# A decoder block on one Trainium2 core: one more column turned by DMA instead of TensorE, and the first turned tile of the mixer's norm joined one weight unit later

## The chip, the cores and the metric

The kernel runs on one core of one Trainium2 chip, and nothing else of the chip is used. The metric is the device time of one execution in microseconds (us); a comparison uses the median of several runs. The core has a matrix engine (TensorE, PE in the profile; PEld is its weight load), a vector engine (VectorE, DVE), an activation engine (ScalarE, ACT), GpSimd (POOL) and SyncE (SP). SP's queue issues all the large transfers. Each engine works through its own instructions in order and waits on semaphores that the others raise.

## The reference, cut to what matters

One layer, batch 1, 256 tokens, model width 2048, feed-forward width 5632, all in float32. `x` is the residual.

```python
def swiglu_ffn(x, w_gate, w_up, w_down):
    return (jax.nn.silu(x @ w_gate) * (x @ w_up)) @ w_down

x = x + 0.5 * swiglu_ffn(rms_norm(x, ffn1_norm), ffn1_w_gate, ffn1_w_up, ffn1_w_down)
z = rms_norm(x, mix_norm) @ w_in                 # 2048 -> 5120 columns
...                                              # RG-LRU branch and short convolution on z
y = concatenate([rms_norm(y_lru, lru_out_norm), rms_norm(y_sc, sc_out_norm)])
x = x + y @ w_out                                # 2048 -> 2048
x = x + 0.5 * swiglu_ffn(rms_norm(x, ffn2_norm), ffn2_w_gate, ffn2_w_up, ffn2_w_down)
return rms_norm(x, final_norm)
```

The change concerns two of these norms: `mix_norm` (called `nm` in the kernel) and `ffn2_norm` (`n2`). Each takes the finished residual, which lies with tokens on the partitions, and needs it turned, with the model dimension on the partitions, because the matrix engine contracts over partitions.

## The kernel before, in words

**Tiling.** The residual `xres` is held on chip as two tiles of 128 tokens (`t` = 0, 1) by 2048 columns, thought of as four columns of 512 (`c` = 0 to 3). A weight unit is a 512 x 512 block of a weight matrix, loaded by one 1 MB transfer from SP's queue (`load`) and cut into a high part (a cast on ACT, `hi_...`, in two halves of 128 x 1024) and a low part (a subtraction on DVE, `lo_...`); three high/low pairs are in use in turn. For two token tiles a unit takes 24 matmuls of 512 columns on PE: 16 with the high part, 8 with the low part. That is done in `multiply`, which ends with a call of `onward()` whenever it works on two targets. The two feed-forward layers use a seven-product scheme (`seven`), and their down projections end with `add_units(3, ...)`.

**Turning a column of the residual.** It is done in one of two ways. `Norm.turn` uses PE: for each of the four blocks of 128 columns two transposes into PSUM (`pt_...`), then one scaling on ACT and one fused multiply-subtract on DVE, which write the high and low part of the turned column `xT_...`. `Norm.cross` uses DMA and is done for each token tile in two steps: `begin` has ACT copy the tile into one side of `pair` as 16-bit halves, and SP issue a transposing DMA from there into a free tile (`cross_...`); `store` has ACT copy the result back (`join`, "COPY pair<-cross" in the trace), and then four scalings on ACT and four multiply-subtracts on DVE write `xT_...`. `pair` has two sides, so two tiles are under way at most.

**What sets the order.** The `cross` tasks lie in the queue `tasks`. Each `onward()`, so each weight unit with two targets, finishes the tile that is under way (`store`) and begins the next one. `Norm.later` puts columns 0 to 2 into that queue and column 3 into `pending` as a `turn` by PE. `pump` and `flush` work `pending` off. Outside a pinned opening, a scheduler reorders the instructions of each engine as it expects them to be ready, so the order on the engines differs from the written one; `join` alone is kept in program order.

**The two places.** The first is the end of the first feed-forward layer, in its last `down`: while the last units of `w_down` (tiles `raw_d1_9_...`) are multiplied, the finished columns of the residual go through `cross_nm_c_t`; `u3` and `s5` there are copies of PSUM sums that ACT takes (`snap`), and PE may reuse a PSUM bank only after such a copy. The mixer's input projection `columns` (sums `ps_in`) follows, and its first unit is followed by the transposes `pt_nm` of column 3. The second place is the start of the second feed-forward layer (`begin_after`): it multiplies four units of `w_gate` and four of `w_up` in turn (`ps_g`, `ps_u`), the first two with `xT` of column 0, the last two with column 3. Column 3 of the residual is complete only after the last unit of `w_out`, right before that loop, and its transposes `pt_n2_12` to `pt_n2_15` stand between the first `ps_g` and the first `ps_u` unit.

Of the kernel before, what the change touches and what calls it, by code (L numbers as in the profile page):

```python
# [12 lines left out]
U16 = mybir.dt.uint16  # L13
# [6 lines left out]
S = 256  # L20
FF = 5632
NT = S // P
KD = D // P
KF = FF // P
CW = 512
NC_D = D // CW
# [23 lines left out]
def hybrid_block(ctx: ExitStack, tc: tile.TileContext, a: dict, out: bass.AP):  # L50
# [3 lines left out]
    x = a["x"][0]  # L54
# [5 lines left out]
    def defer(cost, fn):  # L60
        pending.append((cost, fn))
# [24 lines left out]
    def f32(ap):  # L86
        return ap.bitcast(F32)
# [62 lines left out]
    def big(name):  # L150

        return bigs.tile([P, UK, 2 * S], F32R, tag="big", name=name)
# [42 lines left out]
    def stationary(tile, t):  # L195

        return [(tile[:, j, t * P : (t + 1) * P], tile[:, j, S + t * P : S + (t + 1) * P]) for j in range(UK)]

    mixed, flat = "p (f b) -> p b f", "p (b f) -> p b f"
    pair = const.tile([P, NT, CW], F32, name="pair")  # L200
    tasks, moving, sides = deque(), deque(), [0]

    def part(src, turned):

        sides[0] = 1 - sides[0]
        two = pair[:, sides[0]].bitcast(U16)
        act.copy(two.rearrange(flat, b=2), src.bitcast(U16).rearrange(mixed, b=2))
        nc.sync.dma_start(turned.rearrange("p (r c) -> p r c", c=P), two, transpose=True)
        return pair[:, sides[0]]

    def join(two, turned):
        tc.keep_in_program_order(act.copy(two.bitcast(U16).rearrange(mixed, b=2), turned.rearrange(flat, b=2)))
        return quad(two)

    def onward():

        if moving:
            two, _, fn = moving.popleft()
            fn(two)
        if tasks:  # L220
            key, begin, fn = tasks.popleft()
            moving.append((begin(), key, fn))

    def on_the_way():
        return {task[0] for task in tasks} | {entry[1] for entry in moving}
# [18 lines left out]
    class Norm:  # L244
# [27 lines left out]

        def cross(self, c, t, room):
            x = xres[:, t, c * CW : (c + 1) * CW]
            place = []

            def begin():
                place.append(room(f"cross_{self.name}_{c}_{t}").bitcast(U16))
                return part(x, place[0])

            def store(two):
                v = join(two, place[0])
                if t == 0:
                    self.xT[c] = big(f"xT_{self.name}_{c}")
                for j in range(UK):
                    g = self.gain[:, UK * c + j : UK * c + j + 1]
                    hi, lo = (self.xT[c][:, j, o + t * P : o + (t + 1) * P] for o in (0, S))
                    act.activation(hi, v[:, j], AF.Copy, scale=g)
                    dve.scalar_tensor_tensor(lo, v[:, j], g, f32(hi), op0=ALU.mult, op1=ALU.subtract)

            tasks.append(((self.name, c), begin, store))

        def later(self, c, room):
            if c < NC_D - 1:
                for t in range(NT):
                    self.cross(c, t, room)
            else:
                defer(1.6, lambda: self.turn(range(4 * c, 4 * c + 4)))
            defer(0.1, lambda: self.squares(c))

# [98 lines left out]
    def quad(tile):  # L399
        return tile.rearrange("p (j c) -> p j c", j=UK)  # L400
# [76 lines left out]
    def ffn(tag, norm, after, opening=False):  # L477
        with (
# [37 lines left out]
            def plain(u, x=None):  # L516

                x = f32(norm.xT[u] if x is None else x)
                for t, v in room(u).items():
                    dve.tensor_tensor(  # L520
                        v, x[:, :, t * P : (t + 1) * P], x[:, :, S + t * P : S + (t + 1) * P], op=ALU.add
                    )
# [26 lines left out]
            def first_columns(m, u, **how):  # L549
                return load(ws[m][u * UK * P : (u + 1) * UK * P, :CW], f"{m}{tag}_0_{u}", **how)  # L550
# [136 lines left out]
            def begin_after():  # L687
                follow = {
                    (0, "g"): [flush],
                    (0, "u"): [norm.factor, lambda: plain(0)],  # L690
                    (1, "g"): [lambda: norm.rows(keep), lambda: plain(1), lambda: normalise(0)],
                    (1, "u"): [lambda: normalise(1), sums, lambda: plain(2)],
                    (2, "g"): [lambda: normalise(2), lambda: plain(3)],
                }
                for u in range(KD // UK):
                    for m in "gu":
                        assert (norm.name, u) not in on_the_way()
                        blk = parts_of(first_columns(m, u), f"{m}{tag}_0_{u}")
                        multiply([(ps[m, t], stationary(norm.xT[u], t), u == 0, u == 3) for t in range(NT)], blk)
                        pump(1.5)  # L700
                        for fn in follow.get((u, m), ()):
                            fn()
                units.append(big(f"x{tag}_3"))
                for t in range(NT):
                    sg = keep(f"sg{tag}_0_{t}")
                    act.activation(sg, ps["g", t], AF.Silu, scale=norm.r[:, t : t + 1])
                    dve.scalar_tensor_tensor(
                        sg, ps["u", t], norm.r[:, t : t + 1], sg, op0=ALU.mult, op1=ALU.mult
                    )
                    turn_hidden(0, t, sg, False)  # L710
# [152 lines left out]
    nm = held["nm"]  # L863


    with tc.tile_pool(name="mixer", bufs=1) as mp, tc.tile_pool(name="mixw", bufs=2) as mw:
# [18 lines left out]
        def tmp(tag, name, w=S, dt=F32, bufs=2):  # L885
            return mw.tile([P, w], dt, tag=tag, name=f"{tag}_{name}", bufs=bufs)
# [179 lines left out]
        n2 = Norm("n2", vec["ffn2_norm"])  # L1066
        w_out = a["w_out"][0]
        rs = []
        for c in range(NC_D):
            cs = slice(c * CW, (c + 1) * CW)  # L1070
            for g in range(2):
                if c == 0 and g == 1:
                    flush()
                ps = product(w_out, c, (2 * g, 2 * g + 1), yT.__getitem__, f"o{c}_{g}")
                if c == 0:
                    pst = bank(f"pst_{g}")
                    for t in range(NT):
                        pe.matmul(
                            pst[:, t : t + 1], acc[:, g, t * P : (t + 1) * P], ones[:, :1], start=True, stop=True
                        )  # L1080
                    tot = work.tile([P, NT], F32, tag="tot", name=f"tot_y{g}")
                    dve.tensor_copy(tot, pst[:, :NT])
                    rs.append(inv_sqrt(tot, D // 2, f"y{g}"))
                for t in range(NT):
                    xr = xres[:, t, cs]
                    dve.scalar_tensor_tensor(xr, ps[t], rs[g][:, t : t + 1], xr, op0=ALU.mult, op1=ALU.add)
            n2.later(c, lambda name: tmp("T", name, 4 * S)[:, :CW])


    fss = const.tile([P, NT, NC_D + 1], F32, name="fss")  # L1090
# [87 lines left out]
```

## Time and profile before

| | before |
|---|---|
| median of 3 runs | 1715.81 us (1714.99 to 1716.85) |
| the profiled execution's own time | 1715.85 us |
| its span, first to last instruction | 1713.7 us |
| granted TensorE clock | 0.999 |
| busy, share of the span: PE, PEld | 99%, 82% |
| busy, share of the span: DVE, ACT | 86%, 68% |
| weight transfers, bytes in all, mean rate | 357.91 MB, 209 GB/s |

The profiled execution took 2.15 us more than its span, and 0.04 us more than the median. Busy shares are means over stages. A row of the timeline reads: start in us, time in us, engine, line, operation, output<-inputs, form, count, and in brackets the idle time before it with what ended it. A merged row of several matmuls ends later than the next row starts, because matmuls overlap in the pipeline; the pace of PE is therefore read from one row's start to the next row's start. The profile leaves numbers out of names: `xT_n` of the second layer is `xT_n2`, and `u_d` is one of `u2`, `u3`.

### The profile page before, as it was taken

The page shows a single profiled execution, that of the slowest core. Times are in us where ns is not written, and L with a number is a line of the kernel's source. Part 1 is how long each engine was busy: PE and PEld are TensorE (multiplying, and loading weights), DVE is VectorE, ACT ScalarE, POOL GpSimd, SP SyncE. Part 2 cuts the span into 40 slices and gives each one's busy share as a digit, 9 for nine tenths or more (in the row PEclk, how much of TensorE's full clock was granted, in tenths as well). Part 3 has the DMA queues.
Part 4 walks back from the last instruction along what each step waited for, and adds up shares of the span by engine and source line. Part 5 has one row for each costly group of instructions (what it writes and reads, how often), then busy time and mean ns, then how long its engine had stood idle before and what let it go on. Part 6 is the DMA issues. An engine that isn't in the chain of part 4 may idle for free.

```text
span 1713.7 us, 20224 instructions
## 1 busy us (share of the span) xinstructions
PE 1695.6 (99%) x7811; PEld 1412.7 (82%) x7811; DVE 1479.7 (86%) x1293; ACT 1164.8 (68%) x1481; POOL 6.9 (0%) x32
## 2 busy tenths in 40 slices
PE   8999999999999999999999999999999999999997
PEld 6888888888888887888888888888888888888886
DVE  7998988879889878787987679979989888889796
ACT  6767667776567678875665766686667765677764
POOL 1000000000000000000000000000000000000000
PEclk9999999999999999999999999999999999999999
DMA  8666567585567685755555784695666656576753
GB/s 299 206 220 198 196 221 221 184 268 200 183 209 208 227 264 135 248 172 195 175 195 173 221 278 142 205 269 187 225 202 218 225 186 221 196 215 202 251 192 123
DMA packets 233056, 357.91 MB, mean 209 GB/s; under 512 B 64772, under 2 KB 67200, under 8 KB 232832
## 3 DMA queue, kind: packets, MB, share of 16 engines
q1 hardware_dynamic: 232496, 355.50, 63.8%
q8 instruction: 61, 1.00, 0.2%
q10 hardware_dynamic: 144, 1.05, 0.1%
q14 instruction: 35, 0.29, 0.1%
q0 software_dynamic: 320, 0.07, 0.0%
HBM read 339.82 MB, written 2.10 MB: 200 GB/s over the span
## 4 chain that ended last, share of the span: by engine, by line
PE 75%; ACT 3%; DVE 2%; DMA 0%; issue 0%; DVEq 0%; SPq 0%; ACTq 0%
PE ps_in L43 13%; PE ps_d L43 12%; PE ps_u_a L43 7%; PE ps_g_a L43 6%; PE ps_o L43 5%; PE ps_u_c L43 5%; PE ps_d_a L43 4%; PE ps_g_c L43 3%; PE ps_g_d L43 3%; PE ps_u_d L43 3%; PE ps_d_c L43 2%; PE ps_u_e L43 2%; PE ps_d_d L43 2%; PE ps_g_e L43 2%; PE ps_u L43 1%; PE ps_g L43 1%
## 5 line engine op out<-in xcount | busy, mean ns | idle before, releaser
L43 ACT CAST hi_u_p<-raw_u 128x1024 fp32r<-128x1024 f32 x140 | 141.5, 1047 | 55.7 <-DVE raw_u L43 25.4
L43 ACT CAST hi_g_p<-raw_g 128x1024 fp32r<-128x1024 f32 x132 | 133.9, 1047 | 57.5 <-DVE raw_g L43 30.0
L43 DVE TENSOR_TENSOR lo_u_p<-raw_u,hi_u_p 128x2048 fp32r<-128x2048 f32 (+1 forms) x80 | 159.9, 2018 | 14.4 <-ACT hi_u_p L43 13.8
L43 DVE TENSOR_TENSOR lo_g_p<-raw_g,hi_g_p 128x2048 fp32r<-128x2048 f32 (+1 forms) x75 | 151.6, 2031 | 19.1 <-ACT hi_g_p L43 18.5
L43 PE MATMUL ps_d<-hi_d,h 128*128 128x512 f32 x704 | 167.0, 389 | 0.0
L43 PEld LDWEIGHTS ps_d<-hi_d,h 128*128 128x128 f32 x704 | 132.1, 188 | 27.4
L43 PE MATMUL ps_in<-xT_nm,hi_in 128*128 128x512 f32 x640 | 153.2, 391 | 0.0
L43 PEld LDWEIGHTS ps_in<-xT_nm,hi_in 128*128 128x128 f32 x640 | 117.4, 188 | 23.1 <-ACT tha L43 0.3
L43 ACT CAST hi_d_p<-raw_d 128x1024 fp32r<-128x1024 f32 x84 | 86.1, 1048 | 64.1 <-DVE raw_d L43 24.2
L43 DVE TENSOR_TENSOR lo_d<-raw_d,hi_d 128x2048 fp32r<-128x2048 f32 x44 | 100.2, 2288 | 29.9 <-ACT hi_d L43 29.7
L43 ACT CAST hi_in<-raw_in 128x1024 fp32r<-128x1024 f32 x80 | 80.0, 1045 | 57.5 <-PE ps_in L43 44.5
L43 DVE TENSOR_TENSOR lo_in<-raw_in,hi_in 128x2048 fp32r<-128x2048 f32 x40 | 91.2, 2285 | 31.0 <-ACT hi_in L43 30.6
L43 DVE TENSOR_TENSOR lo_d_p<-raw_d,hi_d_p 128x2048 fp32r<-128x2048 f32 (+1 forms) x48 | 96.5, 2020 | 10.8 <-ACT hi_d_p L43 10.3
L43 ACT CAST hi_u_x<-raw_u 128x1024 fp32r<-128x1024 f32 x80 | 81.3, 1046 | 35.2 <-PE ps_u_c L43 24.9
L43 ACT CAST hi_d<-raw_d 128x1024 fp32r<-128x1024 f32 x88 | 88.9, 1046 | 20.0 <-PE ps_d_d L43 7.6
L43 DVE TENSOR_TENSOR raw_u<-raw_u,raw_u 128x2048 f32<-128x2048 f32 (+1 forms) x50 | 92.3, 1862 | 10.8 <-DMA raw_u<-in_ffn_w_up_dram 10.3
L43 DVE TENSOR_TENSOR lo_g_x<-raw_g,hi_g_x 128x2048 fp32r<-128x2048 f32 x40 | 91.4, 2285 | 8.7 <-ACT hi_g_x L43 8.7
L43 ACT CAST hi_g_x<-raw_g 128x1024 fp32r<-128x1024 f32 x80 | 81.2, 1046 | 21.3 <-PE ps_g_c L43 8.6
L43 DVE TENSOR_TENSOR lo_u_x<-raw_u,hi_u_x 128x2048 fp32r<-128x2048 f32 x40 | 91.4, 2284 | 1.4 <-ACT hi_u_x L43 1.1
L43 DVE TENSOR_TENSOR raw_g<-raw_g,raw_g 128x2048 f32<-128x2048 f32 (+1 forms) x46 | 84.9, 1868 | 5.4 <-DMA raw_g<-in_ffn_w_gate_dram 4.9
L43 PE MATMUL ps_d<-lo_d,h 128*128 128x512 f32 x352 | 87.3, 389 | 0.0
L43 PEld LDWEIGHTS ps_in<-xT_nm,lo_in 128*128 128x128 f32 x640 | 82.1, 191 | 3.1
(406 smaller groups left out, 3669.2 us busy)
## 6 DMA issues: line engine op xcount, KB each, us to landing
raw_d<-in_ffn_w_down_dram SPq DMA_DIRECT2D x88, 1024.0 KB, 5.7
raw_u<-in_ffn_w_up_dram SPq DMA_DIRECT2D x87, 1024.0 KB, 5.3
raw_g<-in_ffn_w_gate_dram SPq DMA_DIRECT2D x86, 1024.0 KB, 5.4
raw_in<-in_w_in_dram SPq DMA_DIRECT2D x40, 1024.0 KB, 5.1
raw_o<-in_w_out_dram SPq DMA_DIRECT2D x16, 1024.0 KB, 5.1
xres<-in_x_dram SPq DMA_DIRECT2D x4, 512.0 KB, 7.7
raw_u<-in_ffn_w_up_dram SPq DMA_DIRECT2D x2, 512.0 KB, 9.5
raw_g_first<-in_ffn_w_gate_dram SPq DMA_DIRECT2D x1, 1024.0 KB, 12.2
```

The lines of the kernel that those rows point to most:

```text
L43: ins = getattr(self.engine, name)(*args, **kwargs)
```

## The change

Three edits. `onward()` skips one call for the very first tile of the mixer's norm (key `("nm", 0)`, seen once): at the unit where that tile would be joined nothing is done, and it and every later tile of the norm come one unit later. `Norm.cross` takes its free tile when the task is queued, no longer when it begins. For `n2`, column 3 is no longer turned on PE: `later` gets `last=False` and leaves out the deferred `turn`, and `begin_after` queues two `cross` tasks for it before its first unit.

```diff
-    tasks, moving, sides = deque(), deque(), [0]
+    tasks, moving, sides, seen = deque(), deque(), [0], set()
...
     def onward():
 
+        if moving and moving[0][3]:
+            moving[0][3] = False
+            return
         if moving:
-            two, _, fn = moving.popleft()
+            two, _, fn, _ = moving.popleft()
             fn(two)
         if tasks:
             key, begin, fn = tasks.popleft()
-            moving.append((begin(), key, fn))
+            moving.append([begin(), key, fn, key == ("nm", 0) and key not in seen])
+            seen.add(key)
...
         def cross(self, c, t, room):
             x = xres[:, t, c * CW : (c + 1) * CW]
-            place = []
+            place = room(f"cross_{self.name}_{c}_{t}").bitcast(U16)
 
             def begin():
-                place.append(room(f"cross_{self.name}_{c}_{t}").bitcast(U16))
-                return part(x, place[0])
+                return part(x, place)
...
-        def later(self, c, room):
+        def later(self, c, room, last=True):
             if c < NC_D - 1:
                 for t in range(NT):
                     self.cross(c, t, room)
-            else:
+            elif last:
                 defer(1.6, lambda: self.turn(range(4 * c, 4 * c + 4)))
             defer(0.1, lambda: self.squares(c))
...
+                for t in range(NT):
+                    norm.cross(NC_D - 1, t, keep)
                 for u in range(KD // UK):
                     for m in "gu":
...
-            n2.later(c, lambda name: tmp("T", name, 4 * S)[:, :CW])
+            n2.later(c, lambda name: tmp("T", name, 4 * S)[:, :CW], False)
```

At the first place, on ACT, before (`cross_nm_0_0` is column 0, token tile 0; `x00`, `p3`, `x10` are three successive weight units; `u3` is a copy of a PSUM sum):

```order
L43 CAST hi_d1_9_p2_4857<-raw_d1_9_101_4684 128x1024
L43 COPY pair_107<-cross_nm_0_0_4772 128x2x512
L43 ACTIVATE xT_nm_0_4825<-pair_107,cols_many_94 128x128 x4
L43 CAST hi_d1_9_x00_4879<-raw_d1_9_70_4688 128x1024 x2
L43 COPY pair_107<-cross_nm_0_1_4834 128x2x512
L43 CAST hi_d1_9_p3_4921<-raw_d1_9_90_4678 128x1024
L43 COPY u3_d1_9_4855<-ps_d1_9_a_4674 128x512
L43 ACTIVATE xT_nm_0_4825<-pair_107,cols_many_94 128x128 x4
```

and now, on ACT at the same place:

```order
L43 CAST hi_d1_9_p2_4845<-raw_d1_9_101_4686 128x1024
L43 CAST hi_d1_9_x00_4869<-raw_d1_9_70_4690 128x1024 x2
L43 COPY pair_107<-cross_nm_0_0_4674 128x2x512
L43 ACTIVATE xT_nm_0_4899<-pair_107,cols_many_94 128x128 x4
L43 CAST hi_d1_9_p3_4911<-raw_d1_9_90_4680 128x1024
L43 COPY u3_d1_9_4843<-ps_d1_9_a_4676 128x512
L43 CAST hi_d1_9_p3_4911<-raw_d1_9_90_4680 128x1024
L43 CAST hi_d1_9_x10_4928<-raw_d1_9_80_4694 128x1024 x2
L43 COPY pair_107<-cross_nm_0_1_4675 128x2x512
```

The two casts of unit `x00` now stand ahead of the first join, and the second join stands behind the copy `u3` and the casts of `x10`, no longer ahead of `u3`.

At the same place on SP's queue, now (before, `cross_nm_0_1` stood right behind `cross_nm_0_0`, and `cross_nm_1_1` right behind `cross_nm_1_0`, each ahead of the weight unit that precedes it now):

```order
L165 DMA raw_d1_9_100_4692<-in_ffn1_w_down_dram 128x4x512
L208 DMA_TRANSPOSE cross_nm_0_0_4674<-pair_107 128x8x128
L165 DMA raw_d1_9_80_4694<-in_ffn1_w_down_dram 128x4x512
L208 DMA_TRANSPOSE cross_nm_0_1_4675<-pair_107 128x8x128
L165 DMA raw_d1_9_3_10_4989<-in_ffn1_w_down_dram 128x4x512
L208 DMA_TRANSPOSE cross_nm_1_0_4867<-pair_107 128x8x128
L165 DMA raw_d1_9_3_9_5044<-in_ffn1_w_down_dram 128x4x512
L208 DMA_TRANSPOSE cross_nm_1_1_4868<-pair_107 128x8x128
```

Two transposing DMAs of this place have moved behind a weight transfer; none was added.

At the second place on PE, before (`ps_g2`, `ps_u2` are the sums of the second layer's first gate and up columns):

```order
L43 MATMUL ps_g2_0_1_8016<-lo_g2_0_0_8022,xT_n2_0_7595 128x512 x4
L43 MATMUL pt_n2_12_8050<-ident_77,xres_76 128x128 x2
L43 MATMUL pt_n2_13_8056<-ident_77,xres_76 128x128 x2
L43 MATMUL pt_n2_14_8061<-ident_77,xres_76 128x128 x2
L43 MATMUL pt_n2_15_8066<-ident_77,xres_76 128x128 x2
L43 MATMUL ps_u2_0_0_8017<-hi_u2_0_0_8077,xT_n2_0_7595 128x512 x8
```

The four rows `pt_n2` are gone from PE, and nothing takes their place there. On ACT, at the same place, now:

```order
L43 COPY pair_107<-xres_76 128x1024
L43 ACTIVATE junk_n2_3_0_8054,ss_n2_7338<-xres_76 128x512
L43 COPY pair_107<-xres_76 128x1024
L43 ACTIVATE junk_n2_3_1_8056,ss_n2_7338<-xres_76 128x512
L43 CAST hi_g2_0_1_8120<-raw_g2_0_1_8118 128x1024
L43 ACTIVATE s_n2_8104<-v_n2_8103 128x2
L43 CAST hi_g2_0_1_8120<-raw_g2_0_1_8118 128x1024
L43 CAST hi_u2_0_1_8179<-raw_u2_0_1_8177 128x1024
L43 COPY pair_107<-cross_n2_3_0_8019 128x2x512
L43 COPY pair_107<-cross_n2_3_1_8020 128x2x512
L43 ACTIVATE xT_n2_3_8090<-pair_107,cols_many_94 128x128 x8
L43 CAST hi_u2_0_1_8179<-raw_u2_0_1_8177 128x1024
```

ACT gained two copies into `pair`, two joins and eight scalings of 128 x 128, and lost four of 128 x 256; the second half of the cast of the second up unit (`hi_u2_0_1`) now stands behind the joins. SP's queue carries the two transposing DMAs between the transfers of `raw_u2_0_1` and `raw_g2_0_2`.

2 lines of the change are left out of this document (1 added, 1 removed).

## The prediction

> **What bounds the kernel now.** I read the page first: the span, the busy shares and the chain that ended last.
>
> ```profile
> span 1713.7 us, 20224 instructions
> PE 1695.6 (99%) x7811; PEld 1412.7 (82%) x7811; DVE 1479.7 (86%) x1293; ACT 1164.8 (68%) x1481; POOL 6.9 (0%) x32
> ```
>
> PE is busy 99%, but busy time alone doesn't say that it is the bound, so next I asked what PE waits for over the whole span (columns: waiter, releaser, us in total, times, longest):
>
> ```profile
> PE pt_n L43 <- DMA xres<-in_x_dram: 3.1, 1, 3.1
> ...
> PE ps_g_a L43 <- DVE lo_g_p L43: 1.4, 4, 0.4
> ...
> PE ps_d_a L43 <- ACT u_d L43: 0.4, 1, 0.4
> ```
>
> After the opening (its longest wait is the 3.1 us), PE waits for nobody longer than half a microsecond at a time. So time is saved only by taking instructions off PE or by removing one of these small waits, and lost only by a new wait of PE. Work added on ACT, DVE or DMA costs nothing until PE waits for it. The last row is at the first place of the change. The chain of waits there, in order of time:
>
> ```profile
> 658.77 8.30 DMA cross_nm<-pair
> ...
> 667.10 1.36 ACT pair L43
> ...
> 673.72 0.58 ACT u_d L43
> ...
> 674.35 2.11 PE ps_d_a L43 x8
> ```
>
> It leaves PE: a transposing DMA takes 8.30 us to land, ACT's join waits for it, everything behind the join on ACT is late, the copy `u_d` among it, and PE stands for that copy.
>
> **The first place: the join one unit later.** ACT's timeline there, then PE's:
>
> ```profile
> 661.79 1.05 ACT L43 CAST hi_d_p<-raw_d 128x1024 fp32r<-128x1024 f32 x1
> 667.10 1.35 ACT L43 COPY pair<-cross_nm 128x1024 uint16<-128x1024 uint16 x1 [4.25 <-DMA cross_nm<-pair]
> ...
> 669.67 1.98 ACT L43 CAST hi_d_x<-raw_d 128x1024 fp32r<-128x1024 f32 x2
> ```
>
> ```profile
> 664.69 1.07 PE L43 MATMUL ps_d_e<-lo_d_x,h 128*128 128x512 f32 x4
> ...
> 666.51 1.98 PE L43 MATMUL ps_d_a<-hi_d_p,hs 128*128 128x512 f32 x8
> ...
> 674.35 2.11 PE L43 MATMUL ps_d_a<-hi_d_x,h 128*128 128x512 f32 x8 [0.42 <-ACT u_d L43]
> ...
> 689.33 3.79 PE L43 MATMUL ps_d<-hi_d,h 128*128 128x512 f32 x16
> ...
> 694.77 3.79 PE L43 MATMUL ps_d<-hi_d,h 128*128 128x512 f32 x16
> ```
>
> The loss is larger than the 0.42 us in brackets, because an interruption also shows as longer steps. The pace is 0.2267 us a matmul: 689.33 to 694.77 is 5.44 us for 24. From 666.51 to 689.33 stand 96 matmuls of 512 columns, that is 21.77 us at this pace, and it took 22.82. So PE loses 1.05 us in this stretch, and that is the most the first edit can bring.
>
> Would it? Now ACT has the casts of unit `x00` between 661.79 and the join. They need the high part of three units earlier, which PE has read by 664.69, so they run from about 664.9 to 666.8, inside the hole of 4.25 us. The join then starts at 667.10 as before, the scalings end at 669.67, the first cast of `p3` at 670.6 and the copy `u3` (one of `u_d`) at 671.1 instead of 674.3. PE wants it at 673.8. What was late is early by more than 2 us, so I take the full 1.05 us. The bounds: 1.05 from above, and from below nothing, or a loss, if the delayed tasks are late at the mixer. The new late candidates come from two transposes now behind a weight transfer on SP's queue. SP's row there (two weight units from 665.19 on), and the landings of the six transposes of this norm:
>
> ```profile
> 665.19 9.17 SPq L165 DMA_DIRECT2D raw_d<-in_ffn_w_down_dram  x2
> ```
>
> ```profile
> DMA to landing us min/median/max: 2.8/4.1/8.3
> ```
>
> The second tile's transpose goes out about 665.6, right behind `raw_d1_9_80`. Even the 8.30 us just seen would land it at 673.9, and its join comes up on ACT at 673.9 by the same durations; behind it the casts of `p1` have until 685.5 on PE. The added wait is thus near nothing; behind it on ACT stand those casts and the two copies for column 1, and DVE's low parts wait for the casts.
>
> At the mixer's start the delayed tasks meet a tight place. SP's, ACT's, DVE's and PE's rows:
>
> ```profile
> 696.05 3.13 SPq L208 DMA_TRANSPOSE cross_nm<-pair  x2
> ```
>
> ```profile
> 700.38 2.57 ACT L43 COPY pair<-cross_nm 128x1024 uint16<-128x1024 uint16 x2 [1.23 <-DMA cross_nm<-pair]
> ```
>
> ```profile
> 704.93 0.69 DVE L43 SCALAR_TENSOR_TENSOR xres<-ps_d,xres 128x512 f32<-128x512 f32 x1
> ```
>
> ```profile
> 703.83 2.08 PE L43 MATMUL ps_in<-xT_nm,lo_in 128*128 128x256 f32 x16
> 705.75 1.03 PE L43 MATMUL pt_nm<-ident,xres 128*128 128x128 f32 x8
> ```
>
> The transposes `pt_nm` read a residual column that DVE finishes at 705.62, queued behind work that waits for ACT's joins of column 2: PE comes at 705.75, only 0.1 us behind. If PE arrives 1.05 us earlier, at 704.70, DVE must be earlier too. Walked through the new order with the same durations, ACT's two copies for column 2 end near 692.7 and 695.2 (the hole of 4.25 us is filled now); before, SP had its first issue only at 696.05. So the second transpose goes out near 695.4, and with the 4.3 us that 696.05 to 700.38 shows it lands near 699.7. One join, one scaling, two multiply-subtracts and the two residual updates are about 3.4 us more: ready at 703.1, with 1.6 us to spare. I keep the full 1.05 for the sum.
>
> **The second place: column 3 of `n2` by DMA.** PE's rows:
>
> ```profile
> 1023.57 1.03 PE L43 MATMUL pt_n<-ident,xres 128*128 128x128 f32 x8
> 1024.36 3.89 PE L43 MATMUL ps_u<-hi_u,xT_n 128*128 128x512 f32 x16
> 1028.08 1.98 PE L43 MATMUL ps_u<-lo_u,xT_n 128*128 128x512 f32 x8
> ...
> 1035.71 3.88 PE L43 MATMUL ps_u<-hi_u,xT_n 128*128 128x512 f32 x16
> ```
>
> The eight transposes hold PE from 1023.57 to 1024.36, 0.79 us, and the 16 matmuls after them take 3.72 instead of 16 x 0.2267 = 3.63, so 0.09 more. Both go: 0.88 us. The Trainium skill ("VectorE: DVE Perf Modes", The three transpose paths) gives 390 ns for a 128x128 transpose on TensorE against 1309 ns by DMA and advises TensorE if PSUM will do as the destination. That advice speaks against this change; by its figure the eight would be an estimated 3.1 us on PE, and the sum below 4.2 instead of 1.93. The rows have 0.79 us for eight, and they decide.
>
> What is added must hide beside PE. Rows for its prices (durations in ns, least/median/most), and ACT's timeline where it goes:
>
> ```profile
> L208 SPq DMA_TRANSPOSE T_cross_n<-pair x6: 1231/1238/1259, 958.7 to 999.3; - x6
> L43 ACT COPY pair<-T_cross_n x6: 1342/1348/1360, 961.7 to 1004.5; 128x1024 uint16<-128x1024 uint16 x6
> DMA to landing us min/median/max: 2.7/2.8/3.2
> L43 ACT ACTIVATE xT_nm<-pair,cols_many x24: 384/388/402, 668.5 to 704.9; 128x128 fp32r<-128x128 f32 x24
> L43 DVE SCALAR_TENSOR_TENSOR xT_nm<-pair,cols_many,xT_nm x24: 341/347/354, 668.9 to 706.3; 128x128 fp32r<-128x128 f32 x24
> L43 DVE SCALAR_TENSOR_TENSOR xT_n<-pt_n,cols_many,xT_n x4: 473/474/477, 1025.6 to 1026.8; 128x256 fp32r<-128x256 f32 x4
> ```
>
> ```profile
> 996.65 1.04 ACT L43 COPY pair<-xres 128x1024 uint16<-128x1024 uint16 x1
> ...
> 1018.41 0.63 ACT L43 ACTIVATE junk_n<-xres 128x512 f32<-128x512 f32 x1
> ...
> 1024.48 1.56 ACT L43 ACTIVATE xT_n<-pt_n,cols_many 128x256 fp32r<-128x256 f32 x4
> 1028.28 2.00 ACT L43 CAST hi_g<-raw_g 128x1024 fp32r<-128x1024 f32 x2 [2.24 <-PE ps_u L43]
> 1033.72 1.99 ACT L43 CAST hi_u<-raw_u 128x1024 fp32r<-128x1024 f32 x2 [3.44 <-PE ps_g L43]
> 1039.13 0.62 ACT L43 CAST x<-v 128x512 fp32r<-128x512 f32 x1 [3.42 <-DVE v L43]
> ```
>
> ACT: 2 x 1.04 + 2 x 1.35 + 8 x 0.39 - 1.56 = +6.3 us. It fits into the 2.24 + 3.44 + 3.42 = 9.1 us in which ACT waits here. DVE: 8 x 0.347 - 4 x 0.474 = +0.9 us, beside a PE that waits for none of it. SP: two issues of 1.24 us; `raw_g2_0_2` behind them leaves about 1 us later, and its cast (the row at 1028.28) waits for PE anyway. The place that could hurt is the cast of `hi_u2_0_1`, half of it behind the joins. The copies for the transposes run from 1018.4 on, with a square between them, so the second transpose goes out near 1021, lands at 1023.7 to 1029.3 (2.7 us to the 8.30 of the first place), and a join (1.35), eight scalings (four step in 1.2, from 668.45 to 669.67 above) and half a cast (1.0), 4.7 us in all, end at 1028.4 to 1034.0. PE wants the cast at 1035.71 - 0.88 = 1034.8. Hidden, with 0.8 us even at the worst landing; I take nothing, and if the cover were gone each further microsecond of landing would be one of PE.
>
> **The sum.** 1.05 + 0.88 = 1.93 us less. The profiled execution took 1715.85 us, so 1713.9 for it; the median, 0.04 lower, gives 1713.88. I predict 1713.9 us, 0.11% less. Of a change under 0.2% (3.4 us) a measurement of this kernel can hardly tell whether there is one: the three runs alone spread over 1.9 us.
>
> **The rivals.** (a) The first place gives nothing back, the second all: the wait moves on, to `cross_nm_0_1` behind its weight unit or to `pt_nm`, whose 0.1 us of slack says that a mixer start no earlier than before eats the 1.05. Then 1715.81 - 0.88 = 1714.9. Against it stands the walk above. This is also the way in which the first edit would not do what it says.
>
> (b) Slower than before: the transposes of column 2, which every delayed task pushes back, land so late that PE stands before `pt_nm`. It is free up to a landing at about 701.3 (704.70 - 3.4); each microsecond beyond is one of PE. From 703.2 on it eats both gains, and from 706.6 on the kernel is over 0.2% slower. Landed at 705, 3.7 us are lost: 1717.6. For it speaks that 8.30 us have been seen for a transpose right behind a weight transfer, and from 695.4 that would be 703.7; against it, the median of the six, 4.1 us.
>
> (c) The second place's transposes land later than 9 us after issue and PE waits for `hi_u2_0_1`; at 12 us, 3 us are lost: 1716.9. Nothing there has taken longer than 3.2 us in the six rows of `T_cross_n`.
>
> (d) DVE is the true bound and its added 0.9 us counts, with PE's relief worth nothing: 1716.7. Against it, PE's waits for DVE's `lo_g_p` sum to 1.4 us over the whole span, none of them here. The Trainium skill ("Perfetto Trace Analysis", Identifying the Most-Contended Engine) calls matmul busy time a poor measure, judges TensorE by its weight-load share instead and names the engine with the highest occupancy as the one to relieve; by that rule DVE's 86% would stand ahead of PEld's 82%. The row of PE's waits disagrees with it here.
>
> **How the numbers follow.** Chances: the full gain 0.60, (a) 0.21, (b) 0.10, (c) 0.04, (d) 0.02, and 0.03 for more than both terms, by a wait elsewhere that the shift dissolves. The full gain gives 1713.9 with 0.9 us to either side for the runs' spread (the three runs' own), so 1713.0 to 1714.8; (a) reaches to 1715.8, and (b) from there up to 1717.6. A range of 1712.8 to 1716.2 takes in the first two and the lower part of (b) and (c), and leaves out less than 2 in 10. Faster by over 0.2% means below 1712.4: 0.04. Slower by over 0.2% means above 1719.2: 0.04, the far end of (b). The rest is within: 0.92.
>
> **What would show it.** In the changed profile: the hole of 4.25 us before ACT's first join gone, the row `ps_d_a` <- `u_d` gone from PE's waits, 96 matmuls in about 21.8 us there; no `pt_n` between the first `ps_g` and `ps_u` of the second layer, and the next unit 24 x 0.2267 = 5.44 us after it; no wait of PE before `pt_nm` or before the second `ps_u`. A bracket of a microsecond or more at one of these, or a new one in the first unit of the mixer, would make the prediction wrong.

## The result, and the profile after

| | before | changed |
|---|---|---|
| median of 21 runs each | 1716.09 us (1714.6 to 1717.76, and one run of 2872.93) | 1713.59 us (1712.3 to 1715.43) |
| ratio, 95% interval | | 0.9985 (0.998 to 0.9991) |
| the profiled execution's own time, its span | 1715.85, 1713.7 us | 1712.30, 1710.3 us |

That is 2.5 us less, and by the interval something between 1.5 and 3.4 us; 1713.9 us was predicted. From here on the first edit is the skip in `onward`, at the first place, and the second edit is the turning of column 3 by DMA, at the second place. The page of the changed kernel:

```profile
span 1710.3 us, 20226 instructions
PE 1693.9 (99%) x7803; PEld 1412.4 (83%) x7803; DVE 1480.0 (87%) x1297; ACT 1169.9 (68%) x1489; POOL 6.9 (0%) x32
```

PE's eight transposes are gone (7811 to 7803), ACT and DVE have eight and four instructions more. What PE waits for, over the whole span (us in total, times, longest):

```profile
PE pt_n L43 <- DMA xres<-in_x_dram: 3.0, 1, 3.0
...
PE ps_g_a L43 <- DVE lo_g_p L43: 1.7, 4, 0.6
PE ps_d_c L43 <- ACT s_d L43: 0.3, 1, 0.3
```

The row `ps_d_a` <- `u_d` is gone, and none has come in its place. The first place, ACT's timeline and then PE's:

```profile
664.06 2.00 ACT L43 CAST hi_d_x<-raw_d 128x1024 fp32r<-128x1024 f32 x2 [2.05 <-PE ps_d_c L43]
665.97 1.36 ACT L43 COPY pair<-cross_nm 128x1024 uint16<-128x1024 uint16 x1
...
669.49 0.57 ACT L43 COPY u_d<-ps_d_a 128x512 f32<-128x512 f32 x1
...
696.80 2.57 ACT L43 COPY pair<-cross_nm 128x1024 uint16<-128x1024 uint16 x2
```

```profile
665.68 1.98 PE L43 MATMUL ps_d_a<-hi_d_p,hs 128*128 128x512 f32 x8
...
672.93 1.98 PE L43 MATMUL ps_d_a<-hi_d_x,h 128*128 128x512 f32 x8
...
687.44 3.79 PE L43 MATMUL ps_d<-hi_d,h 128*128 128x512 f32 x16
...
703.86 1.03 PE L43 MATMUL pt_nm<-ident,xres 128*128 128x128 f32 x8
```

The casts of `x00` fill ACT's former hole, the join has no bracket, `u3` is copied 2.9 us ahead of PE's 672.93 and no longer just behind it, and the 96 matmuls from 665.68 to 687.44 take 21.76 us. The transposes were not made faster: they land after up to 7.7 us still.

```profile
DMA to landing us min/median/max: 2.8/4.9/7.7
```

The second place, PE's rows and ACT's:

```profile
1016.22 3.79 PE L43 MATMUL ps_g<-hi_g,xT_n 128*128 128x512 f32 x16
...
1021.66 3.79 PE L43 MATMUL ps_u<-hi_u,xT_n 128*128 128x512 f32 x16
...
1032.92 3.88 PE L43 MATMUL ps_u<-hi_u,xT_n 128*128 128x512 f32 x16
...
1060.21 1.98 PE L43 MATMUL ps_g_a<-hi_g_p,x 128*128 128x512 f32 x8
```

```profile
1022.61 2.59 ACT L43 COPY pair<-cross_n 128x1024 uint16<-128x1024 uint16 x2
1025.05 2.46 ACT L43 ACTIVATE xT_n<-pair,cols_many 128x128 fp32r<-128x128 f32 x8
1027.39 1.05 ACT L43 CAST hi_u<-raw_u 128x1024 fp32r<-128x1024 f32 x1
```

The gate and the up unit start 5.44 us apart, with nothing between them. The second half of the cast of `hi_u2_0_1` ends at 1028.4, and PE wants it at 1032.9. From the first `ps_g` to the first `ps_g_a` it is 43.99 us; before it was 1063.00 - 1018.12 = 44.88.

One stretch changed that the prediction does not mention, the end. Of each kernel PE's last row, and SP's issue of the last of eight output transfers; before, then changed:

```profile
1703.03 1.07 PE L43 MATMUL ps_d<-lo_d,h 128*128 128x512 f32 x4
```

```profile
1708.94 0.33 SPq L1145 DMA_DIRECT2D out_dram<-xres  x1
```

```profile
1700.58 1.07 PE L43 MATMUL ps_d<-lo_d,h 128*128 128x512 f32 x4
```

```profile
1706.15 0.40 SPq L1150 DMA_DIRECT2D out_dram<-xres  x1
```

From PE's last row the last issue comes after 5.91 and now after 5.57 us, and the span ends after 10.67 and now after 9.72 us. The whole difference of the two spans, 3.4 us, is then: 0.83 ahead of the first place, 1.06 in it, 0.89 at the second place, 0.95 in the end, less 0.34 lost between the second place and the end. Nearly all of the 0.34 is one wait of PE for `lo_g_p`, 0.63 us at 1299.94, where before it was 0.33 at 1302.35. Which of these belong to the change the experiments had to tell.

### The profile page after: what moved, and what is told of

Read it like the earlier page. It is cut to its first block, busy times and chain, and to the rows that moved or that the text cites. A ratio compares the mean times of both kernels' runs of the same rounds, so it can differ in the third digit from the quotient of the medians.

```text
span 1710.3 us, 20226 instructions
## 1 busy us (share of the span) xinstructions
PE 1693.9 (99%) x7803; PEld 1412.4 (83%) x7803; DVE 1480.0 (87%) x1297; ACT 1169.9 (68%) x1489; POOL 6.9 (0%) x32
## 3 DMA queue, kind: packets, MB, share of 16 engines
q10 hardware_dynamic: 144, 1.05, 0.2%
## 4 chain that ended last, share of the span: by engine, by line
PE 92%; ACT 3%; DVE 2%; DMA 1%; issue 1%; SPq 0%; DVEq 0%; ACTq 0%
PE ps_d L43 14%; PE ps_in L43 13%; PE ps_g_a L43 9%; PE ps_u_a L43 8%; PE ps_u_c L43 6%; PE ps_d_a L43 5%; PE ps_o L43 5%; PE ps_g_c L43 5%; PE ps_g_d L43 5%; PE ps_d_c L43 3%; PE ps_u_d L43 3%; PE ps_u_e L43 3%; PE ps_g_e L43 3%; PE ps_d_d L43 3%; PE ps_u L43 2%; PE ps_g L43 2%
```

## Experiments

Four things were read in the same way from each trace, by the starts of PE's rows: the time at which the 96 matmuls begin (everything ahead is the same program in all kernels but the last four, which put a few tiny instructions there), how long those matmuls take, the second place (first `ps_g` to first `ps_g_a`), and the tail, from PE's last row to the end of the span. All times are in us. The diffs are against the changed kernel, those on the tail against the kernel before. The remaining edit, by which `Norm.cross` takes its tile when it is queued, is in every kernel but the one before and those made from it, and was not tried alone. Neither place's gain shows where that place's own edit is missing (22.72 and 44.88 below), so alone it gives neither.

| kernel | 96 begin at | 96 matmuls | second place | tail | median of its runs; before beside it | ratio, 95% interval |
|---|---|---|---|---|---|---|
| before | 666.51 | 22.82 | 44.88 | 10.67 | | |
| before, again | 666.17 | 21.98 | 44.88 | 10.47 | 1716.48; 1716.09 | 1.0 (0.9991 to 1.0009) |
| changed | 665.68 | 21.76 | 43.99 | 9.72 | 1713.59; 1716.09 | 0.9985 (0.998 to 0.9991) |
| changed, again | 666.38 | 21.76 | 43.99 | 9.69 | 1713.55; 1716.09 | 0.9987 (0.9979 to 0.9996) |
| first edit alone | 665.89 | 21.76 | 44.88 | 10.62 | 1714.64; 1716.52 | 0.9992 (0.9983 to 1.0001) |
| second edit alone | 665.78 | 22.72 | 43.99 | 9.71 | 1713.94; 1716.52 | 0.9988 (0.998 to 0.9997) |
| changed + 40 transposes | 666.08 | 21.76 | 48.37 | 9.71 | 1718.27; 1716.52 | 1.0011 (1.0002 to 1.002) |
| changed + 10 adds on DVE | 667.62 | 21.76 | 43.98 | 9.71 | 1714.51; 1716.52 | 0.9992 (0.9983 to 1.0001) |
| shift by two units | 667.41 | 21.76 | 43.99 | 9.75 | 1713.71; 1716.09 | 0.9986 (0.9977 to 0.9996) |
| `nm`'s column 3 by DMA too | 666.51 | 21.76 | 43.98 | 9.64 | 1715.16; 1716.09 | 0.9996 (0.9987 to 1.0004) |
| before + 2 DMAs | 666.70 | 22.90 | 44.88 | 10.30 | 1716.43; 1716.33 | 1.0 (0.9991 to 1.0009) |
| before + 1 DMA | 666.15 | 22.95 | 44.87 | 10.97 | 1715.96 (one run) | |
| before + 8 copies on ACT | 666.66 | 23.05 | 44.89 | 10.60 | 1716.18 (one run) | |
| before + 8 DMAs | 666.08 | 22.80 | 44.89 | 9.92 | 1715.56; 1715.95 | 0.9996 (0.9987 to 1.0005) |

**The first edit alone.**

```diff
-                for t in range(NT):
-                    norm.cross(NC_D - 1, t, keep)
...
-            n2.later(c, lambda name: tmp("T", name, 4 * S)[:, :CW], False)
+            n2.later(c, lambda name: tmp("T", name, 4 * S)[:, :CW])
```

> This kernel has the first edit alone: the first turned tile of the mixer's norm is joined one weight unit later, and column 3 of the second layer's norm goes back to eight transposes on PE. My theory, two independent savings on PE that add up: 1.05 us less than the kernel before (1716.1, so about 1715.0); in the trace the hole of 4.25 us before ACT's first join is gone, the 96 matmuls there take about 21.8 us instead of 22.8, and at the second place the eight transposes are back with their 0.88 us. Rival (a), the wait moves on to the mixer's start: 1716.1, and a wait of PE of about 1 us before pt_nm. Rival, chance: the profile after is 3.4 us shorter than the one before, of which 0.8 us lies ahead of the change; if that belongs to the change, this kernel or the next shows it too, and the two gains sum to 3.4 instead of 1.9.

21.76 us, the transposes back with their 0.88, the tail as before, no wait before `pt_nm`. The medians say 1.9 less, but the interval reaches from 2.9 less to 0.2 more: the trace gives the size, and the runs alone do not even settle the sign.

**The second edit alone.**

```diff
-            moving.append([begin(), key, fn, key == ("nm", 0) and key not in seen])
+            moving.append([begin(), key, fn, False])
```

> This kernel has the second edit alone: column 3 of the second layer's norm is turned by DMA, and nothing is skipped at the end of the first layer. My theory: 0.88 us less than the kernel before (about 1715.2); in the trace no transposes stand between the first gate and the first up unit of the second layer, and that stretch is 0.88 us shorter, while the hole of 4.25 us on ACT, the wait of 0.42 us of PE for the copy u3 and the 22.8 us for 96 matmuls are back. Rival (d), DVE is the bound: 1716.1 + 0.9 = 1717.0. Rival (c), the transposes land late: a wait of PE before the second up unit, 1716 to 1719.

At its place it gives the 0.89 expected, and PE's wait for `u3` is back (0.33 us, 22.72 for the 96). The medians say 2.6 less, though, with an interval from 0.5 to 3.4, and the table shows where more than 0.9 could come from: the tail is 0.9 shorter here as well. It is short in all seven traces with this edit (9.64 to 9.75), and long in every kernel without it and without added DMAs (10.47 to 10.67). The two parts' medians, 1.9 and 2.6, sum to 4.5 where both edits together gave 2.5, which shows how little the medians say about so small a part.

**The two kernels again.**

> The kernel before against itself: a ratio of 1 and a second trace of it. Theory: the stretch of 96 matmuls again 22.8 us, the second layer's start again 44.9 us, since waits there come from the order of the work; the part ahead of the first place differs from the first trace by up to a microsecond, since its waits for the low parts of weights come and go between runs of one program. Rival (they belong to the program): the stall of 0.32 us at 337 us is there again, and PE is again at 545.2 us at the last wait ahead of the change.

> The changed kernel as it is, run a second time beside its parts' rivals. Theory (two savings of 1.05 and 0.88 us, the rest chance): about 1.9 to 2.5 us less than the kernel before, and a second trace in which the two stretches last the same (96 matmuls in about 21.8 us, eight units of the second layer's start in about 44.0 us) while the part of the trace ahead of the first place moves by up to a microsecond. Rival (the 3.4 us between the first two traces all belong to the change): the same 3.4 us again, with the 0.8 us ahead of the first place.

Ahead of the first place the traces differ by up to 1.9 us (665.68 to 667.62) over the same instructions, so the 0.83 there was chance; PE's wait of 0.32 us at 337 us in the first trace of before is absent from the second. The longer wait for `lo_g_p` near 1300 us is in four of the seven traces with the second edit (0.63 to 0.66 us) and not in the other three (0.35 to 0.36), so whether the edit has a part in that 0.34 is open. A surprise is the first place itself. The second execution of the kernel before, ACT and PE:

```profile
665.87 1.36 ACT L43 COPY pair<-cross_nm 128x1024 uint16<-128x1024 uint16 x1 [3.36 <-DMA cross_nm<-pair]
```

```profile
666.17 1.98 PE L43 MATMUL ps_d_a<-hi_d_p,hs 128*128 128x512 f32 x8
...
673.43 1.98 PE L43 MATMUL ps_d_a<-hi_d_x,h 128*128 128x512 f32 x8
...
688.15 3.79 PE L43 MATMUL ps_d<-hi_d,h 128*128 128x512 f32 x16
```

Here the transpose landed after 7.4 us, not 8.3, the join came 0.9 us earlier against PE, and 0.21 us were lost, not 1.05. That loss is thus no constant of the program: in the kernels without the first edit it rises with the landing, up to 1.29 us at 8.5. Over the seven executions without the first edit the stretch takes 22.75 us on average, six times 22.7 to 23.05 and once 21.98, so the edit is worth 0.99.

**What a transpose costs PE.**

```diff
+                        if (u, m) == (0, "g"):
+                            pt = bank("pt_more")
+                            for i in range(40):
+                                k = 12 + i % 4
+                                pe.transpose(pt[:, :P], xres[:, i % 2, k * P : (k + 1) * P], ident)
+                            ...
```

> This kernel is the changed one with 40 transposes of 128x128 added on PE between the first gate unit and the first up unit of the second layer (their results go to a bank of their own, and one column is read once by DVE; the output does not use them). It measures the price that the two readings of the second edit dispute. By the rows of before (eight took 0.79 us from start to next start, 0.099 each): 40 x 0.099 + 0.09 = 4.0 us more than the changed kernel, about 1717.6, and a row of 40 transposes that is 4 us long. By the Trainium skill's 390 ns for one (VectorE: DVE Perf Modes, The three transpose paths): 15.6 us more, about 1729. If PE were not the bound there: less than 1 us more.

```profile
1022.07 4.53 PE L43 MATMUL pt_more<-ident,xres 128*128 128x128 f32 x40
1026.36 3.89 PE L43 MATMUL ps_u<-hi_u,xT_n 128*128 128x512 f32 x16
```

From start to start 4.29 us, 0.107 each, and the second place grows by 4.38. The median is 1.75 us above the kernel before, where the changed kernel's, in its own two batches, is 2.5 below it: 4.25 in all. Each microsecond put on PE there is one of time, and the estimate from the Trainium skill's figure (15.6 us) is far off.

**What more work on DVE costs.**

```diff
+                        if (u, m) == (0, "g"):
+                            more = work.tile([P, P], F32, tag="more", name="more", bufs=1)
+                            for i in range(10):
+                                x3 = [xres[:, t, D - P :] for t in range(NT)]
+                                dve.tensor_tensor(more, x3[0], x3[1], op=ALU.add)
```

> This kernel is the changed one with ten adds of 128x128 on DVE at the second place, about 0.28 us each by the shape, 2.8 us in all (results unused), three times the 0.9 us by which the second edit loads DVE. My theory, DVE is covered by PE here: within 0.3 us of the changed kernel (about 1713.6). Rival (d), DVE is the bound: 2.8 us more, about 1716.4, with PE waiting for DVE behind that place.

PE's rows behind the second place, first of the changed kernel, then of the one with the adds; the last row is the adds' durations on DVE in ns:

```profile
1060.21 1.98 PE L43 MATMUL ps_g_a<-hi_g_p,x 128*128 128x512 f32 x8
...
1073.36 1.13 PE L43 MATMUL ps_g_a<-lo_g_p,xs 128*128 128x512 f32 x4
...
1077.50 1.07 PE L43 MATMUL ps_g_e<-lo_g_x,x 128*128 128x512 f32 x4
```

```profile
1062.15 1.98 PE L43 MATMUL ps_g_a<-hi_g_p,x 128*128 128x512 f32 x8
...
1076.15 1.20 PE L43 MATMUL ps_g_a<-lo_g_p,xs 128*128 128x512 f32 x4 [0.23 <-DVE lo_g_p L43]
...
1079.91 1.07 PE L43 MATMUL ps_g_e<-lo_g_x,x 128*128 128x512 f32 x4
...
1109.83 0.73 PE L43 MATMUL ps_u_c<-lo_u_p,xs 128*128 128x512 f32 x2 [1.10 <-DVE lo_u_p L43]
```

```profile
L43 DVE TENSOR_TENSOR more<-xres x10: 282/285/293, 1021.2 to 1028.2; 128x128 f32<-128x128 f32 x10
```

At the second place itself they cost nothing (43.98). Some 45 us behind the adds, though, PE waits for DVE's `lo_g_p`, and DVE has hardly a gap from there back to the adds. The same 76 matmuls, from the first `ps_g_a` row to the last `ps_g_e` row shown, take 17.76 us with the adds, 17.29 in the changed kernel and 17.29 to 17.31 in the seven traces without the second edit, so about 0.5 of the 2.85 us is paid there. (The rows `ps_g_a<-lo_g_p,xs` can't be compared: with the adds two more matmuls stand ahead of it.) At 1109.83 PE waits another 1.10 us. DVE had stood 2.75 us for a weight transfer just before, and in the kernel before with two and with eight DMAs added, which has no adds, PE waits 0.57 and 0.62 us at the same matmul; how much of the 1.10 the adds cost is open.

The first of these waits also comes without any adds. In the kernel with the shift by two units, below:

```profile
1061.94 1.98 PE L43 MATMUL ps_g_a<-hi_g_p,x 128*128 128x512 f32 x8
...
1075.66 1.21 PE L43 MATMUL ps_g_a<-lo_g_p,xs 128*128 128x512 f32 x4 [0.41 <-DVE lo_g_p L43]
...
1079.91 1.07 PE L43 MATMUL ps_g_e<-lo_g_x,x 128*128 128x512 f32 x4
```

That is 17.97 us; the kernel with `nm`'s column 3 by DMA too has 17.98, and the changed kernel's second trace 17.49. What these three share is a late join: ACT's first join of column 3 begins 6.81, 7.11 and 6.68 us behind the first `ps_g`, and DVE then stands 0.7, 1.0 and 0.5 us for ACT's scalings. In the three traces that lose next to nothing (the changed kernel's first, the second edit alone, the 40 transposes) the join begins at 6.35 to 6.39 and DVE stands 0.2 to 0.3. No run moved the join alone, so this link is read from six traces and not tried. The cover behind the second place is thin, then: it holds for the second edit's 0.9 us when the joins are in time, and neither for three times as much on DVE nor, in these traces, for joins 0.3 to 0.7 us later. "Within 0.3 us" was too good, and rival (d) is true in part, beyond the cover. The runs (2.0 us below before, the changed kernel 2.5 below in its own two batches) cannot tell this apart.

**The shift by two units.**

```diff
-            moving[0][3] = False
+            moving[0][3] -= 1
...
-            moving.append([begin(), key, fn, key == ("nm", 0) and key not in seen])
+            moving.append([begin(), key, fn, 2 * (key == ("nm", 0) and key not in seen)])
...
             onward()
+            if u == 0 and name == "in_0_0":
+                onward()
```

> The changed kernel with the first turned tile joined two units later, not one; one more onward() behind the mixer's first unit catches up. It asks how much room the shift had. Theory: the copy u3 stays early, so the 96 matmuls take 21.8 us as with one unit; but column 2 is joined 5.4 us (one unit) later, about 10 us after PE's first unit of the mixer begins, where 12 us are there: no gain over one unit, 1713.6, or up to 2 us of waiting of PE before the mixer's third unit: 1715.6. Rival (rival b of the prediction, PE stands before pt_nm): 4 us or more, 1717 and above.

```profile
702.06 2.58 ACT L43 COPY pair<-cross_nm 128x1024 uint16<-128x1024 uint16 x2 [2.21 <-DMA cross_nm<-pair]
```

ACT now does wait for column 2, but PE passes `pt_nm` without a wait: in this order DVE updates the residual ahead of the multiply-subtracts that depend on the join. No gain and no loss against one unit (1713.71 and, in the same batch, 1713.55). Rival (b) itself was not reached: PE comes to `pt_nm` at 705.59 here, so by the rival's own price a landing is free up to 705.59 - 3.4 = 702.2, and this one was in by 702.06. But the residual was done at 703.4, where that price would have had it at 705.5; in this order (b) begins later than its price said.

**The same edit at the mixer's norm.**

```diff
-            held["nm"].later(c, held["keep"])
+            held["nm"].later(c, held["keep"], False)
...
+        for t in range(NT):
+            nm.cross(NC_D - 1, t, lambda name: tmp("T", name, 4 * S)[:, :CW])
+        onward()
```

> The same edit at one more place: the changed kernel, and column 3 of the mixer's norm is turned by DMA too (two more tasks behind column 2, and one more call of onward() at the mixer's start to make room for them). Theory: the eight transposes pt_nm leave PE, 0.79 + 0.09 us less than the changed kernel (about 1712.7), if the joins are done before PE wants the fourth unit, about 12 us after the residual column is complete at 701.5: copies 2.1, a landing of 3 to 8, two joins 2.7, scalings and multiply-subtracts about 3, so 10.8 to 15.8 us after it. Rival: late, and PE waits up to 3 us in the fourth unit of the mixer: 1713 to 1716.

The transposes go and the joins are in time, but PE then stands elsewhere:

```profile
727.42 2.46 PE L43 MATMUL ps_in<-xT_nm,hi_in 128*128 128x512 f32 x10
730.87 0.38 PE L43 MATMUL pgate_a<-xs,gate_a 128*128 128x256 f32 x1 [1.00 <-ACT xs L43]
```

On ACT the casts of the gate weights begin at 715.98, behind the joins, where they stood at 708.72 in the changed kernel's second trace. DVE's low parts of them follow, DVE has no gap from 716 to 733, and `xs` is late. From the mixer's first matmul to the first `ps_g` it is 318.28 us, where the changed kernel has 317.87 and 317.90: the 0.88 of the transposes is in it, so 1.3 are lost again, and this stretch is worse by 0.4. The wait that goes with late joins, above, costs this trace 0.7 more behind the second place. The runs are worse by 1.6 in the same batch and spread wider (1712.89 to 1717.4); the profiled execution took 1713.57, 1.6 less than their median, so where the rest goes is open.

**The tail.** SP's part of it was tried by adding DMAs of 64 bytes to the kernel before, and ACT's by eight small copies:

```diff
+                pad = const.tile([1, 64], F32, name="pad")
+                for i in range(2):
+                    nc.sync.dma_start(pad[:, 16 * i : 16 * i + 16], ones[:1, :16])
```

> The kernel before with two DMAs of 64 bytes added on SP's queue at the second place; nothing reads them. In the traces so far the time from PE's last row to the end of the span is 10.5 to 10.7 us in the three kernels without the second edit and 9.6 to 9.75 in the six with it, while the arithmetic there lasts the same; and a packet of instructions is fetched 1 to 2 us behind the last output transfer without that edit, and some 3 us ahead of it with it. Theory: the 0.9 us come from SP's count of instructions, which the edit's two DMAs raise; then this kernel has a tail of 9.6 to 9.8 us and an earlier packet, no other stretch changes, and it is 0.9 us faster than before (1715.2 beside 1716.1). Rival: the 0.9 us come from ACT's or DVE's added instructions, or from the transposes themselves: the tail stays at 10.5 to 10.7 us.

> The kernel before with one DMA of 64 bytes added on SP's queue at the second place. It asks whether the tail moves by steps. Theory: what counts is on which side of the last output transfer the fetch of the packet falls, so the tail is either that of the kernel before (10.5 to 10.7 us) or that of the changed one (9.6 to 9.8 us), with the packet behind or ahead of the last transfer accordingly. Rival, each added DMA takes its share: 10.1 to 10.2 us.

> The kernel before with eight small copies (128x2) added on ACT at the second place, as many instructions as the second edit adds on ACT; nothing reads them. Theory (SP's count of instructions sets the tail): the tail stays at 10.5 to 10.7 us. Rival (ACT's count does): 9.6 to 9.8 us.

> The kernel before with eight DMAs of 64 bytes added on SP's queue, where two and one were added in the last runs. There a gap of about 0.3 us in SP's issuing of the last four output transfers moved forward with each count: ahead of the fourth in the kernel before (4.56, 5.10, 5.91 us behind PE's last row), ahead of the third with one and with two added (4.55, 5.40, 5.85), nowhere in the changed kernel (4.57, 5.08, 5.57). Theory (a stop at a fixed number of SP's instructions, with its fetch beside the output): eight move it ahead of all four, where SP waits anyway; the last issue is then at about 5.6, the tail 9.6 to 9.8 us, and the time 0.9 us less than the kernel before. Rival (it is not the count but what the second edit's transposes are): the gap stays among the four and the tail at 10.3 us or more.

The scheduler put the copies at 2 us and the DMAs at 28 us and later, not at the second place; the last output transfers come far behind either. ACT's copies change nothing (10.60), so the count of ACT's instructions is not the cause. One and two DMAs did not give the tail expected, but the single issues, in us behind PE's last row, show what moves:

| kernel | 4th issue | 5th | 6th | 7th | 8th | tail |
|---|---|---|---|---|---|---|
| before | 0.20 | 4.18 | 4.56 | 5.10 | **5.91** | 10.67 |
| before + 1 DMA | 0.20 | 4.19 | 4.56 | **5.40** | 5.85 | 10.97 |
| before + 2 DMAs | 0.19 | 4.18 | 4.55 | **5.40** | 5.84 | 10.30 |
| before + 8 DMAs | 0.19 | 4.18 | 4.56 | 5.09 | 5.58 | 9.92 |
| changed | 0.18 | 4.17 | 4.57 | 5.08 | 5.57 | 9.72 |
| `nm`'s column 3 by DMA too | **0.51** | 4.18 | 4.58 | 5.09 | 5.58 | 9.64 |

An issue that comes 0.3 us late (bold) moves forward the more SP has issued before: from the eighth to the seventh, in the changed kernel out of sight (between the fourth and the fifth SP waits anyway), and with two more transposes to the fourth. A packet of instructions is fetched near it: 1.6 us behind the late issue in the kernel before (1.2 in its second trace), 3 us ahead of the last issue in the changed kernel, 29 us ahead with eight DMAs. With eight the last issue is at 5.58 and the tail 0.55 to 0.75 shorter than in the two traces of before, against the rival of the last expectation. So the change's shorter tail goes with what SP has issued before it, for the most part, and needs no transposes; that two transposes move the late issue further than two plain DMAs is not explained. Of the 0.95 us between the first two traces, 0.34 is the late issue; the remaining 0.6 lies between the last issue and the end (4.76 to 4.15 us) and goes with the fetch in these traces, but by what mechanism isn't shown, and why the tail is 10.97 with one DMA and 10.30 with two is open. In the runs' time, the kernel with eight DMAs is 0.4 us below before, which the interval doesn't tell from 0.9 or from nothing.

## Why the prediction was right

**First place, 1.05.** Right in mechanism and size: 1.06 between the first two traces, 0.99 on average over seven executions without the edit. What the prediction took as fixed, the loss of 1.05, is one point of a slope: 0.21 with a landing of 7.4 us, 1.05 with 8.3. The walk was right in its rows: casts 664.06 (664.9 predicted), `u3` at 669.49 (671.1), the last residual update done at 701.5 (703.1), `pt_nm` reached by PE at 703.86 (704.70), where this trace begins the place 0.83 earlier than the first; the slack ahead of `pt_nm` was 2.4 us, not 1.6.

**Second place, 0.88.** 0.89 in every trace with the edit that adds nothing there. At the place itself what was to hide the added work hid it: no new bracket on PE, and `hi_u2_0_1` done 4.5 us before PE wants it, where the walk had 0.8 to 6.4. The transposes landed after 4.1 and 4.9 us. What the prediction did not price is DVE's next tight row, some 57 us behind the place's start: with joins 0.3 to 0.7 us later than in the first trace, 0.2 to 0.7 us of the gain are lost again there (0.2 in the changed kernel's second trace). The price of a transpose was taken from the row, 0.099 us each, and forty take 0.107 each; the Trainium skill's 390 ns ("VectorE: DVE Perf Modes", The three transpose paths; given there for bf16, where these are f32) does not hold for transposes in a row of matmuls. The Trainium skill's advice to use TensorE if PSUM will do (same page, Rules for kernel authors) did not pay here, and for another reason than the price: each microsecond on PE was one of time, while the work added on the other engines was covered at the place.

**The sum, 1.93.** Its two terms sum to 1.87 or 1.88 by the tables. A third term, the 0.9 us of the tail, is missing from it: the step that should have seen it is "SP: two issues of 1.24 us", which counted their time at the place and not that they shift SP's later instructions against the output transfers. With it the sum is 2.8 us, and 2.5 was measured, interval 1.5 to 3.4. The runs alone do not decide between 1.9 and 2.8; that the term exists is read from the traces, all seven of which have it. That 1713.9 came within 0.3 us of 1713.59 is in part luck: reckoned from the median of 21 runs, 1716.09, the two terms give 1714.16, so the low median of the first three runs made up half of the 0.57 us by which the sum fell short.

**The rivals.** (a) fell: the wait did not move on, in any trace with the first edit. (b) did not come, even with the shift doubled. (c) did not come as described: no wait for `hi_u2_0_1`, with landings of 3.8 to 5.7 us over the seven traces. But its bound of 9 us was too kind, because in the three traces whose slower landing took 5.1 to 5.7 us PE already lost 0.2 to 0.7 us further on. (d) fell for the edit's 0.9 us when the joins are in time, and came true in part for 2.85. Judged by weight-load share alone, as the prediction took the Trainium skill's rule ("Perfetto Trace Analysis", Identifying the Most-Contended Engine; the Trainium skill names the share of peak matmul work beside it), DVE at 87% against PEld's 83% would still be the engine to relieve. Yet forty transposes on PE cost their whole 4.3 us, and ten adds on DVE about 0.5 of their 2.85 at the row where PE next needed it.

## What to carry to other kernels

Where one engine is busy 99% of the time, price an edit by what it takes off that engine from row start to row start, and price what it adds elsewhere by the slack at the row where the bound engine next needs it, which can lie 45 us behind the edit. A stall found in one trace may be a slope that another execution meets lower down, so read a second trace before its size is taken for granted. And when several traces differ, cut them at the same rows first, and count that the same matmuls lie between them: of 3.4 us between two spans here, the edits' own places explained 1.9 and the program's end 0.9; most of the rest was chance ahead of the first place.

## What was not expected of the hardware

The same instructions took up to 1.9 us more or less to reach the first place at 666 us. Over the traces the transposing DMA of one tile landed after 2.7 to 8.5 us at the first place and after 3.8 to 5.7 us at the second. And SP's issues have a stop of about 0.3 us that moves forward the more SP has issued before it: with the stop among the last two output transfers the tail is 10.30 to 10.97 us, in the other kernels 9.64 to 9.92.
